# Pinning the order of every engine at the border between the up and the down projection of an encoder layer

## The chip, the cores and the metric

The kernel runs on one core of one Trainium2 chip. The metric is the device time of one execution in microseconds (us); lower is better. Engines are named as the profile names them: PE (TensorE, matrix products; PEld is its weight load), DVE (VectorE), ACT (ScalarE), POOL (GpSimd) and SP (SyncE, which here only issues DMA transfers).

## The reference, cut to what matters

One layer of a streaming encoder: a mixer (two kinds of attention, a gated MLP, an output projection, LayerNorm) and then the part that this document is about, a squared-ReLU MLP with a residual and a LayerNorm, on 1024 prompt tokens and 64 sample tokens, in float32:

```
def sq_relu_mlp(x, w_up, w_down):
    h = jnp.square(jax.nn.relu(jnp.einsum('btd,df->btf', x, w_up)))
    return jnp.einsum('btf,fd->btd', h, w_down)

xp = layer_norm(ALPHA * xp + sq_relu_mlp(xp, w_up[l], w_down[l]), ln2_g[l], ln2_b[l])
```

D_MODEL is 1024 and D_FF 4096, so w_up is 1024 x 4096 and w_down 4096 x 1024.

## The kernel before, in words

Both projections use Strassen-Winograd products: seven products in place of eight for a 2 x 2 split of rows, columns and depth. Each float32 operand is held as two halves of a rounded type, hi and lo: `split` (L1180 on) has ACT write hi, and DVE or POOL write lo = raw - hi. Every product takes three passes (hi x hi, hi x lo, lo x hi).

**The up part** runs over 16 pairs p of 256 columns of w_up. A pair has two token halves s, of 288 columns (s = 0, which carries half of the sample) and 256 columns (s = 1). One pair and half is a `Chain` (L1223): `product(i)` for i = 0 to 6 issues 12 matmuls into a PSUM bank A, B, C or D (the table PROD, L1219) and what takes the bank out. I write (14,1).6 for product 6 of pair 14, half 1. Products 0, 2 and 4 add up in bank A, and ACT copies the bank out after each of them (L1251), so product 2 waits for the copy after product 0, and product 4 for the copy after 2. Product 1 is added by DVE to the first copy (L1253). After product 5 DVE makes out(5) from bank D and the third copy (L1255), and out(3) from the third copy and bank C (L1256). Product 6 adds to bank D, so it waits for out(5); DVE then makes out(4) (L1258). `finish` (L1261) squares the four sums in place (L1265), makes four differences (L1271 to L1274), and SP stores the eight blocks to DRAM (h4_dr, h3_dr, hs_dr; L1275 to L1279). The copies lie in a tile `sn` of three slots, the blocks in a tile `hh`; each half has its own (tags sn0, sn1, hh0, hh1), and the next chain with that tag waits until the stores have read it. `prep(p)` loads a pair of w_up into the tile tagged `wr` and makes its operands; the x operands of half 1 lie in two tiles of the pool `big` (tag xw), those of half 0 in xo0.

**The down part** runs over 16 groups g = 2c + part. A group takes two pairs of h (q = 0, 1) against one row block of w_down (index c) for two token blocks x. `Down.product(n)` issues six matmuls of 512 columns, `Down.evac(n)` takes the bank out: ACT for n = 0 (L1587), DVE into the accumulators `acc` else (L1535, L1537, L1580). For each c and q, `wd_load` brings 1 MB of w_down (two transfers of 512 KB) into a raw tile, `wd_split` n = 0 to 6 makes seven hi and lo pairs (wset[0] lies in the two tiles `slots`, which take the place of the x operands of half 1; wset[1] lies in the pool dp on the right side, which is laid over what the up part used there), and `wd_sums` makes four differences in the raw tile between them. `h_load` brings h back from DRAM (into `awa` for the four-block part, `hr` for the three-block part), `h_split` makes its hi on ACT (L1396), copies it to PSUM on ACT (L1400), and has DVE write lo (L1401). `acc_load` loads the accumulators, which start as the mixer's result. `sample(c)` (L1614, L1616) does the sample tokens.

**What sets the order.** Each engine runs its instructions strictly in its own order, and a waiting instruction holds all behind it; so does SP with its transfers. A scheduler orders the instructions of the program when the kernel is built, from its own estimate of their times, with the earlier written ones preferred. `in_order()` (L99) is an exception: it links all instructions written inside it, engine by engine (SP too), in the order written. Before the change only the last part (c = 7 and the final LayerNorm, L1745 on) is pinned in this way.

**Around the border** (L1456 to L1502): after `prep(15)` the code writes chain (14,1), products 0 to 3 of (14,0), chain (15,1), then the allocation of `slots`, both `wd_load(0, q)` (q = 0 into `wr`, q = 1 into `hh1`), products 4 to 6 of (14,0), splits and sums, the loads of h and of accumulator 0, and chain (15,0) with more splits between its products. The loop of groups follows, all of it left to the scheduler. In the final part, `put_gb` (four ACT copies, L1728) stands before `squares(5)` (one ACT instruction with a sum, L1648), and `on_dve(5, ...)` (L1679, L1681) between the evacuations of the third chain.

## Time and profile before

| what | value |
|---|---|
| median of 3 runs | 1437.42 us (1433.44 to 1439.77) |
| profiled execution, its own time | 1441.04 us |
| its span in the profile | 1439.3 us |
| PE busy | 1340.2 us, 93% of the span |
| DVE, ACT, POOL busy | 1010.3, 720.3, 610.5 us |
| mean granted TensorE clock | 0.965 |
| up part, first and last matmul | 675.3 to 1063 us |
| down part, first and last matmul | 1044.9 to 1429 us |

The profile is of one execution, on the core's own time axis from the start of the span. A line of the timeline gives start, duration, engine, line of the program, operation, output and inputs by tile name, a count of merged instructions, and in brackets the idle time ahead of it with what ended it. A table by windows gives, for stretches of time, the length, the busy time and number of instructions per engine, then the mean granted clock of PE (1.00 is full), the share of the DMA engines and their GB/s. Merged matmul rows can carry the form of one of the two chains that they hold.

### The profile page before, as it was taken

What the parts mean: (1) busy time and instruction counts of PE and PEld (TensorE: products, weight loads), DVE (VectorE), ACT (ScalarE), POOL (GpSimd) and SP (SyncE); (2) the same over time, 40 slices, a digit from 0 to 9 for tenths busy, and PEclk for the clock granted to TensorE, in tenths of its full rate; (3) what the DMA queues carried; (4) which work ended last, traced back from release to release, by engine and by line L of the source; (5) the groups of instructions that cost most, each with busy time, mean ns of one, the idle gap of its engine ahead of it and who ended that gap; (6) DMA issues with size and microseconds to landing.
All of it is one profiled execution on the core that took longest, in us unless ns stands there. A gap on an engine that the chain in (4) does not pass through costs nothing.

```text
span 1439.3 us, 24229 instructions
## 1 busy us (share of the span) xinstructions
PE 1340.2 (93%) x8827; PEld 1217.8 (85%) x8827; DVE 1010.3 (70%) x1802; ACT 720.3 (50%) x1561; POOL 610.5 (42%) x660
## 2 busy tenths in 40 slices
PE   7999999999989988989879999999969999999996
PEld 6899999998988986867779999999947787787874
DVE  3567565767885699786736877876678667777766
ACT  3366565666564675233323222223335757667664
POOL 2222323266563537664322221222254556565555
PEclk9999999999999998989989999999978999999997
DMA  7324232322213434331124434334475334344433
GB/s 213 78 77 110 61 110 65 82 58 65 64 31 84 128 103 154 118 106 41 57 85 165 151 128 163 136 117 161 163 256 176 121 139 139 133 142 137 138 110 117
DMA packets 146208, 168.60 MB, mean 117 GB/s; under 512 B 27036, under 2 KB 112348, under 8 KB 146088
## 3 DMA queue, kind: packets, MB, share of 16 engines
q1 hardware_dynamic: 146088, 167.04, 37.0%
q8 instruction: 70, 1.15, 0.3%
q14 instruction: 50, 0.41, 0.1%
HBM read 109.00 MB, written 51.71 MB: 112 GB/s over the span
## 4 chain that ended last, share of the span: by engine, by line
PE 67%; DVE 9%; DMA 7%; ACT 7%; POOL 4%; issue 4%; SPq 1%; DVEq 0%; ACTq 0%; POOLq 0%
PE zA L1242 9%; PE mx L232 7%; PE zD L1242 6%; PE A L1570 6%; PE kvsb L337 5%; PE kvfox L337 4%; PE zB L1242 3%; PE zC L1242 3%; PE D L1570 3%; PE qsb L478 2%; DMA rd<-w_down 2%; PE qfox L478 2%; POOL wd L97 2%; PE Sfox L536 2%; PE B L1570 1%
## 5 line engine op out<-in xcount | busy, mean ns | idle before, releaser
L97 POOL TENSOR_TENSOR wa<-wr,wa 128x512 fp32r<-128x512 f32 x45 | 68.8, 1556 | 230.3 <-ACT wa L1182 230.3
L97 POOL TENSOR_TENSOR wd<-rd,wd 128x512 fp32r<-128x512 f32 x80 | 108.5, 1371 | 100.8 <-ACT wd L1182 96.5
L232 PE MATMUL mx<-xT,oTb 128*128 128x512 f32 (+1 forms) x416 | 108.8, 415 | 3.0 <-ACT oTb L191 2.0
L1242 PE MATMUL zA<-xo,ws 128*128 128x288 f32 (+1 forms) x720 | 96.7, 289 | 2.5 <-ACT sn L1251 2.5
L1242 PE MATMUL zD<-xo,ws 128*128 128x288 f32 (+1 forms) x720 | 98.3, 291 | 0.0
L232 PEld LDWEIGHTS mx<-xT,oTb 128*128 128x128 f32 (+1 forms) x416 | 78.7, 194 | 23.0 <-ACT oTb L191 2.9
L1251 ACT ACTIVATE sn<-zA 128x288 f32<-128x288 f32 (+1 forms) x96 | 37.7, 393 | 119.0 <-PE zA L1242 105.7
L1242 PEld LDWEIGHTS zA<-xo,ws 128*128 128x128 f32 x720 | 93.4, 189 | 3.0 <-ACT sn L1251 2.9
L1182 ACT ACTIVATE wd<-rd 128x512 fp32r<-128x512 f32 x112 | 67.6, 623 | 55.6 <-DMA rd<-w_down 25.1
L1242 PEld LDWEIGHTS zD<-xo,ws 128*128 128x128 f32 x720 | 94.9, 191 | 0.2
L337 PE MATMUL kvfox<-wkvfox,xT 128*128 128x256 f32 (+3 forms) x624 | 91.0, 295 | 3.1 <-DVE fx L440 2.0
L522 POOL TENSOR_TENSOR sgsb<-sgsb,snsb 128x127 f32<-128x127 f32 (+7 forms) x48 | 58.8, 1227 | 78.5 <-DVE snsb L520 67.6
L1570 PE MATMUL A<-wd,wd 128*128 128x512 f32 x312 | 86.9, 406 | 4.2 <-DVE acc L1537 3.4
L337 PE MATMUL kvsb<-wkvsb,xT 128*128 128x256 f32 (+1 forms) x624 | 87.7, 286 | 0.0
L337 PEld LDWEIGHTS kvfox<-wkvfox,xT 128*128 128x128 f32 (+1 forms) x624 | 82.1, 195 | 4.7 <-DVE fx L440 2.2
L1371 POOL TENSOR_TENSOR rd<-rd 128x512 f32<-128x512 f32 x56 | 79.8, 1425 | 10.7 <-DVE b L97 8.3
L520 DVE TENSOR_TENSOR_SCAN snsb<-snsb,one 128x128 f32<-128x128 f32 (+7 forms) x48 | 72.1, 1506 | 13.3 <-ACT snsb L519 12.7
L337 PEld LDWEIGHTS kvsb<-wkvsb,xT 128*128 128x128 f32 (+1 forms) x624 | 79.2, 187 | 0.2
L1570 PEld LDWEIGHTS A<-wd,wd 128*128 128x128 f32 x312 | 60.2, 195 | 20.7 <-issue 3.6
L1570 PE MATMUL A<-wd,h4a 128*128 128x512 f32 x240 | 68.3, 406 | 9.7 <-POOL wd L97 3.6
L1570 PEld LDWEIGHTS A<-wd,h4a 128*128 128x128 f32 x240 | 45.9, 193 | 22.8 <-POOL wd L97 4.4
L1438 ACT ACTIVATE ws<-wr 128x1024 fp32r<-128x1024 f32 x30 | 31.2, 1057 | 58.4 <-DVE wr L1192 58.4
(511 smaller groups left out, 3751.7 us busy)
## 6 DMA issues: line engine op xcount, KB each, us to landing
rd<-w_down SPq DMA_DIRECT2D x32, 512.0 KB, 4.4
awa<-h_dr SPq DMA_DIRECT2D x32, 512.0 KB, 4.3
wr<-w_up SPq DMA_DIRECT2D x15, 1024.0 KB, 5.5
h_dr<-hh SPq DMA_DIRECT2D x30, 512.0 KB, 3.2
hr<-h_dr SPq DMA_DIRECT2D x32, 384.0 KB, 3.5
h_dr<-hh SPq DMA_DIRECT2D x30, 384.0 KB, 3.5
raw<-w_in SPq DMA_DIRECT2D x44, 256.0 KB, 3.5
xr<-x_prompt SPq DMA_DIRECT2D x8, 512.0 KB, 6.9
```

Source lines behind the costliest of these rows:

```text
L97: eng.tensor_tensor(out, src, hi.bitcast(F32), op=ALU.subtract)
L232: nc.tensor.matmul(acc[0:m], oT[:, k, hx, 0:m], wo[k // 4][hw][:, k % 4, cs], start=(i == 0), stop=(i == len(seq) - 1))
L337: nc.tensor.matmul(acc[0:n, c0:c0 + n1 - n0], xT[k // 4][:, k % 4, c:c + n], wt[:, k, hw, n0:n1], start=(i == 0), stop=(i == len(seq) - 1))
L478: nc.tensor.matmul(acc[:, 0:w], wq[:, k, hw, :], xT[k // 4][:, k % 4, c:c + w], start=(i == 0), stop=(i == len(seq) - 1))
L520: nc.vector.tensor_tensor_scan(g[:, 0:n][:, ::-1], g[:, 0:n][:, ::-1], one.broadcast_to([P, n]), 1.0, op0=ALU.mult, op1=ALU.bypass)
L522: nc.gpsimd.tensor_tensor(s[:, 0:n - 1], s[:, 0:n - 1], g[:, 1:n], op=ALU.mult)
L1182: nc.scalar.activation(hi, raw, AF.Copy)
L1242: nc.tensor.matmul(z, w[:, hw, k], xop(s, bo, hx)[:, k, :], start=(new and k == 0 and j == 0), stop=(k == 3 and j == 2), skip_group_check= ...
L1251: nc.scalar.activation(sn[:, (0, None, 1, None, 2)[i], 0:n], z, AF.Copy)
L1371: eng.tensor_tensor(r[:, o], r[:, x], r[:, y], op=ALU.subtract)
L1438: nc.scalar.activation(ws[:, 0, q], raw[:, q], AF.Copy)
L1570: nc.tensor.matmul(z, h[:, hx, q, o], wset[self.c % 2][q][:, hw, wb], start=((n in (0, 3) or n == 1 and self.c == 0) and q == 0 and j == 0 ...
```

## The change

`in_order` gets an optional dictionary, so that a second pinned block goes on behind a first one on every engine. The border is one such block and the first group of down another, on the same dictionary.

Within the border the four chains run one behind another: (14,1), (15,1), (14,0), (15,0), with the last product of each put behind the first product of the next one. Chains of both halves alternate between the tag sets: (14,1) and (14,0) use sn1 and hh1, (15,1) and (15,0) use sn0 and hh0. `sn` has two slots in place of three, in all chains of the up part; the third copy is written by ACT straight to out(0) in `hh`. Both `wd_load(0, q)` go through `wr`, the second one behind the last split of the first. For q = 0 POOL does five of seven lo halves and DVE two; for q = 1 POOL does all seven. The first group of down is written out with its loads, splits and the last `finish`; the loop starts at g = 1, `sample(0)` moves from g = 0 to g = 1, and the operands `b12` of the sample are loaded by transfers of their own for c = 0 and for (1, 0) in g = 1.

In the final part `squares(5)` moves ahead of `put_gb`, each `on_dve(5, ...)` moves back by one place, and the small statistics tiles lie in the identity matrix, which is no longer needed by then.

```diff
     @contextmanager
-    def in_order():
+    def in_order(prev=None):
 
         traced = nc.cur_bb.bb.instructions
         last = traced[-1]
         yield
         at = next(k for k in reversed(range(len(traced))) if traced[k] is last) + 1
-        prev = {}
+        prev = {} if prev is None else prev
         for i in traced[at:]:
             p = prev.get(i.engine)
             if p is not None:
...
-        def product(self, i):
...
             if b == "A":
-                nc.scalar.activation(sn[:, (0, None, 1, None, 2)[i], 0:n], z, AF.Copy)
+
+                nc.scalar.activation(out(0) if i == 4 else sn[:, i // 2, 0:n], z, AF.Copy)
             elif b == "B":
                 add(out(2), z, sn[:, 0, 0:n], op=ALU.add)
             elif i == 5:
-                add(out(5), self.bank["D"], sn[:, 2, 0:n], op=ALU.add)
-                add(out(3), sn[:, 2, 0:n], z, op=ALU.subtract)
+                add(out(5), self.bank["D"], out(0), op=ALU.add)
+                add(out(3), out(0), z, op=ALU.subtract)
             elif i == 6:
                 add(out(4), z, sn[:, 1, 0:n], op=ALU.add)
-                self.finish(n)
-
-        def finish(self, n):
+                if rest:
+                    self.finish()
+
+        def finish(self):
             p, s = self.p, self.s
+            n = NS[s]
             for a, b in self.runs:
...
     def first_chain(s, weave):
-        sn = [sp.tile([P, 288], F32, name=f"sn0_{s}_{q}", tag="gl", bufs=3) for q in range(3)]
-
-        class Three:
...
     def wd_sums(c, q, eng):
 
+        for k in range(4):
+            wd_sum(c, q, k, eng)
+
+    def wd_sum(c, q, k, eng):
         r = raws[c, q]
-        for o, x, y in ((0, 1, 0), (1, 3, 1), (3, 3, 0), (2, 2, 3)):
-            eng.tensor_tensor(r[:, o], r[:, x], r[:, y], op=ALU.subtract)
+        o, x, y = ((0, 1, 0), (1, 3, 1), (3, 3, 0), (2, 2, 3))[k]
...
-            tag = only or ("o", "tr")[n_stage[0] % 2]
+            tag = (only or ("o", "tr"))[n_stage[0] % 2]
             n_stage[0] += 1
-            st = ps.tile([P, 4, P], F32, name=f"st{n_stage[0]}", tag=tag, bufs=1)[:, 0:o]
...
-        def chain(p, s):
-            sn = lp.tile([P, 3, NS[s]], F32, name=f"sn{p}_{s}", tag=f"sn{s}")
-            h8 = lp.tile([P, 8, NS[s]], F32, name=f"hh{p}_{s}", tag=f"hh{s}")
+        def chain(p, s, at=None):
+            at = s if at is None else at
+            sn = lp.tile([P, 2, NS[0]], F32, name=f"sn{p}_{s}", tag=f"sn{at}")
+            h8 = lp.tile([P, 8 * NS[0]], F32, name=f"hh{p}_{s}", tag=f"hh{at}")[:, 0:8 * NS[s]].rearrange(
+                "p (b c) -> p b c", b=8)
             return Chain(p, s, sn, lambda a, b: h8[:, a:b], ((2, 6),))
...
         prep(NP - 1)
-        c1, c0 = chain(NP - 2, 1), chain(NP - 2, 0)
-        for i in range(7):
-            c1.product(i)
-        for i in range(4):
-            c0.product(i)
...
+        q4 = [chain(NP - 2, 1, 1), chain(NP - 1, 1, 0)]
+        border = {}
+        with in_order(border):
+            for i in range(6):
+                q4[0].product(i)
+            wd_load(0, 0, "wr")
+            q4[1].product(0)
+            q4[0].product(6)
+            for i in range(1, 6):
+                q4[1].product(i)
+            q4.append(chain(NP - 2, 0, 1))
+            q4[2].product(0)
+            q4[1].product(6)
+            slots = [big.tile([P, 8704], F32R, name=f"wd0_{q}", tag="xw") for q in range(2)]
             for q in range(2):
-                wd_split(0, q, n, nc.gpsimd)
-        for q in range(2):
-            wd_sums(0, q, nc.vector)
-        h4 = lp.tile([P, 2, 2, 2, 4, P], F32R, name="h4a", tag="ws")
-        hbuf[0, 0], hbuf[0, 1] = h4[:, 0], h4[:, 1]
-        awa = lp.tile([P, 3, D], F32, name="awa", tag="wa")
-        hraw[0, 0], hraw[0, 1] = (awa[:, q].rearrange("p (o c) -> p o c", o=4) for q in range(2))
-        two(0, awa[:, 2])
-        for q in range(2):
-            h_load(0, 0, q)
-        h_load(0, 1, 1)
-        acc_load(0)
-        c0 = chain(NP - 1, 0)
-        for i in range(7):
-            c0.product(i)
-            if i in (0, 1, 2, 3):
-                for q in range(2):
-                    wd_split(0, q, i + 3, (nc.gpsimd, nc.vector)[q])
-            if i in (2, 4):
-                h_split(0, 0, i // 2 - 1, "tr")
-            if i == 4:
-                a45 = lp.tile([P, 2, D], F32, name="acc45", tag="hh1")
-                two(1, a45[:, 0])
-                two(4, a45[:, 1])
-                acc_load(1)
-                acc_load(4)
-            if i == 6:
-                h_load(0, 1, 0)
+                wset[0][q] = slots[q][:, 0:7168].rearrange("p (h b c) -> p h b c", h=2, b=7)
+                hbuf[1, q] = slots[q][:, 7168:8704].rearrange("p (h q o c) -> p h q o c", h=2, q=2, o=3)
+            q4[2].product(1)
+            wd_split(0, 0, 0, nc.gpsimd)
+            wd_split(0, 0, 2, nc.vector)
+            q4[2].product(2)
+            wd_sum(0, 0, 0, nc.vector)
+            wd_split(0, 0, 1, nc.gpsimd)
+            q4[2].product(3)
+            wd_sum(0, 0, 1, nc.vector)
+            wd_sum(0, 0, 2, nc.vector)
+            wd_split(0, 0, 4, nc.vector)
+            q4[2].product(4)
+            wd_sum(0, 0, 3, nc.vector)
+            wd_split(0, 0, 3, nc.gpsimd)
+            q4[2].product(5)
+            wd_split(0, 0, 5, nc.gpsimd)
+            wd_split(0, 0, 6, nc.gpsimd)
+            wd_load(0, 1, "wr")
+            q4.append(chain(NP - 1, 0, 0))
+            q4[3].product(0)
+            q4[2].product(6, False)
+            h4 = lp.tile([P, 2, 2, 2, 4, P], F32R, name="h4a", tag="ws")
+            hbuf[0, 0], hbuf[0, 1] = h4[:, 0], h4[:, 1]
+            awa = lp.tile([P, 3, D], F32, name="awa", tag="wa")
+            hraw[0, 0], hraw[0, 1] = (awa[:, q].rearrange("p (o c) -> p o c", o=4) for q in range(2))
+            two(0, awa[:, 2])
+            for q in range(2):
+                h_load(0, 0, q)
+            acc_load(0)
+            q4[2].finish()
+            h_load(0, 1, 1)
+            q4[3].product(1)
+            q4[3].product(2)
+            h_split(0, 0, 0, ("tr", "pt"))
+            q4[3].product(3)
+            wd_split(0, 1, 0, nc.gpsimd)
+            wd_split(0, 1, 1, nc.gpsimd)
+            q4[3].product(4)
+            h_split(0, 0, 1, ("tr", "pt"))
+            a45 = lp.tile([P, 2, D], F32, name="acc45", tag="hh1")
+            two(1, a45[:, 0])
+            two(4, a45[:, 1])
+            acc_load(1)
+            acc_load(4)
+            wd_sum(0, 1, 0, nc.vector)
+            wd_split(0, 1, 2, nc.gpsimd)
+            q4[3].product(5)
+            wd_sum(0, 1, 1, nc.vector)
+            wd_sum(0, 1, 2, nc.vector)
+            wd_split(0, 1, 3, nc.gpsimd)
+            q4[3].product(6, False)
+            h_load(0, 1, 0)
+            wd_split(0, 1, 4, nc.gpsimd)
+            wd_sum(0, 1, 3, nc.vector)
+            wd_split(0, 1, 5, nc.gpsimd)
+            wd_split(0, 1, 6, nc.gpsimd)
...
@@ -1512,18 +1548,6 @@
         for t in (5, 3, 7, NB):
             two(t, dp.tile([P, D], F32, name=f"acc{t}"))
         hs = dp.tile([P, 2, 2, 2, TS], F32R, name="hs")
-        a26 = lp.tile([P, 2304], F32, name="acc26", tag="hh0")
-        two(2, a26[:, 0:D])
-        two(6, a26[:, D:2 * D])
-        hsr = a26[:, 2 * D:2304].rearrange("p (q o c) -> p q o c", q=2, o=4)
-        for t in (5, 2, 6, 3, 7, NB):
-            acc_load(t)
-        for q in range(2):
-
-            r = dp.tile([P, 512], F32, name=f"rb{q}", tag="p1", bufs=2)
-            nc.sync.dma_start(r, w_dn[2 * q * P:(2 * q + 1) * P, 512:D])
-            split(b12[q][:, 0], b12[q][:, 1], r, nc.gpsimd)
-        hs_load(0)
...
         def norm(t):
             if t not in lst:
-                lst[t] = dp.tile([P, 16], F32, name=f"lstb{t}", tag="lst", bufs=NT)
+
+                lst[t] = ident[:, 16 * t:16 * t + 16] if t < NB else dp.tile([P, 16], F32, name="lstb")
             return lst[t]
...
+        def b12_again(c, q):
+
+            r = dp.tile([P, 512], F32, name=f"rb{c}_{q}", tag="p1", bufs=2)
+            k = 2 * (2 * c + q)
+            nc.sync.dma_start(r, w_dn[k * P:(k + 1) * P, 512:D])
+            split(b12[q][:, 0], b12[q][:, 1], r, nc.gpsimd)
+
+        def first_group():
+            ch = [Down(0, x) for x in range(2)]
+
+            def both(n):
+                for d in ch:
+                    d.product(n)
+                for d in ch:
+                    d.evac(n)
+
+            acc_load(5)
+            for q in range(2):
+                h_load(1, 0, q)
+            both(0)
+            q4[3].finish()
+            both(1)
+            wd_load(1, 0)
+            h_split(0, 1, 0)
+            both(2)
+            h_split(0, 1, 1)
+            for q in range(2):
+                h_load(1, 1, q)
+            both(3)
+            for k in range(3):
+                wd_split(1, 0, k, nc.gpsimd)
+            for t in (2, 6, 3, 7, NB):
+                acc_load(t)
+            h_split(1, 0, 0)
+            both(4)
+            wd_sums(1, 0, nc.gpsimd)
+            both(5)
+            h_split(1, 0, 1)
+            wd_split(1, 0, 3, nc.vector)
+            wd_split(1, 0, 4, nc.gpsimd)
+            both(6)
+            wd_split(1, 0, 5, nc.vector)
+            wd_split(1, 0, 6, nc.gpsimd)
+
+        a26 = lp.tile([P, 2304], F32, name="acc26", tag="hh0")
+        two(2, a26[:, 0:D])
+        two(6, a26[:, D:2 * D])
+        hsr = a26[:, 2 * D:2304].rearrange("p (q o c) -> p q o c", q=2, o=4)
+        with in_order(border):
+            first_group()
         for c in range(NC - 1):
             for part in range(2):
                 g = 2 * c + part
+                if g == 0:
+                    continue
+                if g == 1:
+                    hs_load(0)
+                    for q in range(2):
+                        b12_again(0, q)
                 wd_load(c + 1, part)
                 ch = [Down(g, x) for x in range(2)]
...
-                    if n == 3 and part == 0:
+                    if n == 3 and (part == 0 or g == 1):
                         sample(c)
+                        if g == 1:
+                            b12_again(1, 0)
...
@@ -1800,21 +1883,21 @@
             shift(1)
             do(2, 1)
             h_split(g + 1, 1, 1)
+            squares(5)
             put_gb()
-            squares(5)
             normalize(1)
             times(1)
             do(2, 2)
-            on_dve(5, 0, 0)
             ch[3].preload()
             do(2, 3)
+            on_dve(5, 0, 0)
+            do(2, 4)
             on_dve(5, 1, 0)
-            do(2, 4)
-            on_dve(5, 0, 1)
             do(2, 5)
             neg_mean(2)
+            on_dve(5, 0, 1)
+            do(3, 0)
             on_dve(5, 1, 1)
-            do(3, 0)
             squares(2)
```

## The prediction, made before the changed kernel had run

> **What bounds the kernel now.** I read the engine shares first, then the stretches of the border, then each engine's timeline there.
>
> ```profile
> PE 1340.2 (93%) x8827; PEld 1217.8 (85%) x8827; DVE 1010.3 (70%) x1802; ACT 720.3 (50%) x1561; POOL 610.5 (42%) x660
> PEclk9999999999999998989989999999978999999997
> PE 67%; DVE 9%; DMA 7%; ACT 7%; POOL 4%; issue 4%; SPq 1%; DVEq 0%; ACTq 0%; POOLq 0%
> ```
>
> PE bounds nearly all of it, and from 1100 to 1380 us it is busy for 279.3 of 280 us. What another order can give is PE's idle time and its lowered clock. The stretches of the border (length, busy us and count on PE, PEld, DVE, ACT, POOL, then clock, DMA share, GB/s):
>
> ```profile
> 1030.00:1045.00 15.00, 15.00 (x118) 15.00 (x118) 10.63 (x13) 7.62 (x16) 8.91 (x6) 1.00 0.40 133
> 1045.00:1060.00 15.00, 7.47 (x39) 5.92 (x38) 9.76 (x18) 4.38 (x10) 2.96 (x2) 0.91 0.76 261
> 1060.00:1075.00 15.00, 9.00 (x27) 6.81 (x27) 10.63 (x9) 7.22 (x14) 11.18 (x8) 0.61 0.96 313
> 1075.00:1090.00 15.00, 12.04 (x32) 8.49 (x31) 13.08 (x17) 7.54 (x15) 6.34 (x6) 0.57 0.69 245
> 1090.00:1100.00 10.00, 10.00 (x45) 7.73 (x44) 7.25 (x12) 3.82 (x8) 4.28 (x5) 1.00 0.25 86
> ```
>
> From 1045 to 1090 us there are 98 matmuls: 37 of up (288 columns, 24 in 3.04 us, so 0.127 each) and 61 of down (512 columns, 6 in 1.40 us, 0.23 each). At full clock they take 4.7 + 14.0 = 18.7 us; they took 45. So **26.3 us** are lost there. The waits behind it, and the second lossy place, at the end:
>
> ```profile
> 1059.09 1.65 PE L1570 MATMUL B<-wd,h4a 128*128 128x512 f32 x3 [4.08 <-DVE hh L1253]
> 1072.34 2.07 PE L1570 MATMUL A<-wd,h4a 128*128 128x512 f32 x4 [3.63 <-POOL wd L97]
> 1082.01 2.93 PE L1570 MATMUL A<-wd,h4a 128*128 128x512 f32 x6 [2.42 <-ACT p L1587]
> 1409.64 2.90 PE L1570 MATMUL A<-wd,wd 128*128 128x512 f32 x6 [3.18 <-DVE acc L1537]
> 1413.17 2.93 PE L1570 MATMUL lastD<-wd,wd 128*128 128x512 f32 x6 [0.63 <-DVE acc L1537]
> ```
>
> Six matmuls take 2.7 us there in place of 1.4: half clock. The weights came late because the heads of two queues stood waiting for (15,0).6 with splits of already landed weights behind them, on ACT and on POOL:
>
> ```profile
> 1063.71 1.67 ACT L1182 ACTIVATE wd<-rd 128x512 fp32r<-128x512 f32 x3 [8.92 <-PE zD L1242]
> 1063.74 0.95 POOL L1414 MEMSET acc<- 64x1024 f32 x1 [15.79 <-PE zD L1242]
> ```
>
> In two-microsecond stretches (PE busy, clock, DMA share, GB/s) the clock shows when it steps:
>
> ```profile
> 1057.00:1059.00 2.00, 0.00 (x0) 0.58 1.00 307
> 1063.00:1065.00 2.00, 1.62 (x6) 0.71 0.68 178
> 1067.00:1069.00 2.00, 1.71 (x4) 0.64 0.93 323
> 1087.00:1089.00 2.00, 2.00 (x8) 0.74 1.04 394
> ```
>
> Read as a mix of 1.00 and 0.50 these put the steps at 1057.3 (down), 1064.2 (up), 1067.6 (down) and 1088.0 (up): multiples of 3.4 us apart. A 3.4 us window in which PE was busy for 28 to 33% ended in half clock, windows of 47 and 54% did not, and it took a fully busy window to come back (one of 81 to 84% did not do it). So a gap costs itself, and if some 2.2 us of it fall in one window, another 1.7 to 3.4 us after it (half of 3.4 to 6.8 us), 2.6 on average.
>
> **The change, part by part.** Times below are on the trace's axis; after 1007.3 us, where (14,1) starts, they are forecasts. A product of 12 takes 1.42 us with 256 columns, 1.52 with 288.
>
> *The third copy goes to out(0).* ACT now has to wait for hh1, whose stores by (13,1) were issued late:
>
> ```profile
> 1014.84 0.33 SPq L1275 DMA_DIRECT2D h_dr<-hh  x1
> 1015.78 0.33 SPq L1276 DMA_DIRECT2D h_dr<-hh  x1
> 1030.57 0.42 DVE L1253 TENSOR_TENSOR hh<-zB,sn 128x256 f32<-128x256 f32 x1 [3.31 <-DMA h_dr<-hh]
> ```
>
> The last row resumed 3.28 us after its store's issue (1027.29), so hh1 is free at 1019.1. Then the copy (0.39), two DVE adds (0.42 each, partly beside it) and (14,1).6 can go at 1020.4. Before, products of (14,0) filled this; now six products and (15,1).0 end at 1017.4. **Gap 1: 3.0 us**, with 6 in 10 chances that 2.2 us of it fall in one window, so I add 2.6. Bounds: 0 (the stores land sooner, 2.1 us being the shortest such transfer here, and DVE is not behind) to 8 (DVE takes the waiting add ahead of the 7.5 us in which it makes the operands of pair 15). The Trainium skill, TensorE: Matmul & The Clock Gate, section Part 1, says that PE falls to half clock after at least one idle window of some 3.4 us; by that, gap 1 would stay warm and the sum come out 2.6 us better. The rows above differ: a window that was 28% busy was enough.
>
> *The chains one behind another.* (15,1).6 then ends at T = 1020.4 + 11.5 + 2.6 = 1034.5, and `slots` is free. From T: POOL's and DVE's work for q = 0 is a chain, since a sum waits for a split's lo and a later split for the sum. POOL needs 1.3 us per lo alone (1.29 in the last group), and a DVE operation with both inputs in SBUF waits while POOL has one: the four differences of (15,0) took 1.37 to 1.50 us beside POOL, 0.41 elsewhere. `finish` of (15,1) on DVE goes to T+3.7, sums 1 and 2 to 7.9, sum 3 to 9.1; POOL's five end at 6.1 (second), 10.4, 11.7, 13.3. So out(5) of (14,0) is ready at 9.5 where PE is at 9.1: 0.5 us, and (14,0).6 ends at 11.1.
>
> *Loads.* SP is pinned: `wd_load(0, 1)` needs `wr`, free at T+13.3 (1047.8; before, it went to hh1 at 1047.98), and `h_load(0, 0, q)` stands behind it, though `awa` is free at 11.2. The first `wd_load` before (1 MB, issued 1019.8) had its bytes moved from 1021 to 1024. So w_down moves from T+14.7 to 17.8, h to 21.0. Then ACT, in its pinned order: hi, copy, hi, copy for x = 0 (0.55 each), two splits of q = 1, the copy after (15,0).4, four more for x = 1: T+26.2. DVE then: the last lo (0.7), a sum (0.6), out(5): **(15,0).6 starts at T+28.1**. PE's other work ends at 11.1 + 5 x 1.52 = 18.7. **Gap 2: 9.4 us, and 2.6** of half clock behind it. Lower bound 6 (loads as quick as the 4.3 us median, no collisions of DVE and POOL), upper 14 (each DVE difference at 1.4 us).
>
> *The first group.* Its weights for n = 0 and 1 are there, the others come from POOL by T+38 in the order of use. DVE is the tight one: out(4), a sum, `finish` (7.5 us for (15,0) beside a busy POOL, 1063.7 to 1071.2), then evacuations and lo halves; (n = 4) needs them at T+44.6 and gets them at 44.6. SP's queue holds stores, accumulators and h ahead of `wd_load(1, 0)`; it lands at T+45 and is needed in g = 2. For evacuations that come just late I count 1.5 us; bounds 0 and 5.
>
> *Costs at nothing.* POOL does two more lo halves and two more of b12, 6 us in some 45 of which it is busy about 30. The 16 sample matmuls only move. One load of 256 KB more: DMA is under half busy after 1100 us. Two slots of `sn`: the same instructions; in pair 0 the 3.35 us wait at 716.5 for the stores of the first chain can grow by one copy, 0.4 us.
>
> *The final part.* `squares(5)` (1.13 us) no longer waits for `put_gb` (2.32 us), and DVE evacuates (2,3) before it meets `on_dve(5, 0, 0)`, which waited 2.27 us for `squares(5)`. The 3.18 us gap stays (its evacuation stands behind `h_split`, unmoved); the 0.63 us gap goes, and with it the broken window that kept the clock at half from 1409.6 to 1419.1 (4.75 us lost). Left: 2.6. Gain 0.6 + 2.2 = **2.8 us**; bounds 0.6 and 4. The work moved back falls into DVE's idle 2.64 us at 1420.
>
> **Sum.** After: 3.0 + 2.6 + 0.5 + 9.4 + 2.6 + 1.5 = 19.6 lost, before 26.3: 6.7, and 2.8 at the end: 9.5 us. Against the profiled execution's 1441.0 that is 1431.5; it lies 3.6 above the median of 1437.4, from which I get 1427.9.
>
> **Rivals.** (a) *Gaps close further*: gap 1 stays warm, gap 2 is 6 us, the first group runs through: 2.6 + 3.4 + 1.5 more, 1420. For it: DMA reached over 400 GB/s in stretches of the trace. Of this, that gap 1 alone leaves the clock up has a chance of 0.4, since it falls across two windows that often, and gives 9.5 + 2.6 = 12.1 us, 1425.3, within the forecast's own range. (That is also what the clock rule of the Trainium skill, TensorE: Matmul & The Clock Gate, Part 1, would make of it.) (b) *The wait is only moved*: hh1 late with DVE's order against it (5 more) and gap 2 at 13: 9.5 - 8.6, 1436.5. For it: DVE and POOL did collide in every difference of (15,0). (c) *Slower*: the first group never gets warm. Before, gaps of 0.5 to 3.6 us kept half clock from 1067.6 to 1088.0; if DVE's evacuations, pinned behind `finish` and the lo halves, leave a gap of 0.6 us in each window, its 84 matmuls take 38.6 us in place of 19.3. That is 16.7 beyond the 2.6 counted, plus five gaps: 9.5 - 19.7, 1447.6. It decides once evacuations lag PE by over 1.4 us. Against it: some 19 us of DVE work stand in 24.
>
> **How the numbers follow.** About 0.5% (7.2 us) can be told from no change here. Forecast 0.48 (1423 to 1434, two thirds of it past 0.5%), (a) 0.26, (b) 0.13, (c) 0.13. Faster 0.32 + 0.26 = 0.58, same 0.16 + 0.13 = 0.29, slower 0.13. Range 1417 (all low bounds, less 3 of scatter) to 1438 (gap 1 at 8, gap 2 at 14).
>
> **What would show it.** Right: a PE gap near 3 us ended by out(0)'s copy or out(5) before (14,1).6, the long gap before (15,0).6 with h's loads in its chain, full clock through most of g = 0, no 0.63 us gap near the end. Wrong: h landed before (15,0).3, so that gap 2 is short; or gaps inside g = 0; or g = 2 waiting for weights.

## The result and the profile after

The changed kernel takes 1428.53 us (median of 6 runs, 1426.93 to 1430.65), the kernel before 1437.24 (6 runs): ratio 0.9943, 95% interval 0.9922 to 0.9964. A second comparison, beside later experiments, gave 1430.31 against 1438.94: 0.9948 [0.9931, 0.9966]. So it is 7.5 to 8.7 us faster, where 9.5 was forecast. The profiled execution took 1429.89 us (span 1428.2); that of before 1441.04.

Engine shares, clock and chain of waits of after:

```profile
PE 1333.8 (93%) x8827; PEld 1214.6 (85%) x8827; DVE 1001.7 (70%) x1799; ACT 720.9 (50%) x1561; POOL 613.6 (43%) x663
PEclk9999999999999998999979999999999999999998
PE 61%; DVE 11%; DMA 8%; ACT 7%; POOL 6%; issue 6%; SPq 1%; DVEq 0%; ACTq 0%; POOLq 0%
```

The mean clock went from 0.965 to 0.970, and PE's busy time fell by 6.4 us with the same 8827 matmuls: fewer of them ran at half clock. The stretches of the border (columns as before):

```profile
1030.00:1045.00 15.00, 15.00 (x116) 14.87 (x115) 10.32 (x17) 5.47 (x11) 6.04 (x5) 1.00 0.16 63
1045.00:1060.00 15.00, 9.12 (x58) 8.64 (x56) 6.40 (x11) 6.72 (x13) 3.52 (x3) 0.79 0.81 270
1060.00:1075.00 15.00, 12.87 (x61) 10.53 (x60) 14.58 (x19) 6.01 (x13) 8.43 (x5) 0.98 0.79 274
1075.00:1090.00 15.00, 12.48 (x52) 9.48 (x53) 10.20 (x17) 11.58 (x23) 10.64 (x9) 1.00 0.97 329
1090.00:1100.00 10.00, 10.00 (x45) 8.19 (x44) 10.00 (x18) 7.79 (x16) 6.38 (x6) 1.00 0.71 251
```

Between 1060 and 1090 us the clock was 0.61 and 0.57 before and is 0.98 and 1.00 now. PE's gaps in the border and in the final part, from PE's timeline:

```profile
1020.20 2.93 PE L1242 MATMUL zD<-xo,ws 128*128 128x256 f32 x12 [2.94 <-DVE hh L1256]
1056.85 3.25 PE L1242 MATMUL zC<-xo,wa 128*128 128x288 f32 x12 [5.88 <-DVE h4a L1408]
1061.53 1.86 PE L1242 MATMUL zD<-xo,ws 128*128 128x288 f32 x12 [1.43 <-DVE hh L1256]
1076.01 0.93 PE L1594 MATMUL A<-wd 128*128 128x512 f32 x3 [1.71 <-DVE awa L1559]
1083.62 0.97 PE L1594 MATMUL A<-wd,h4b 128*128 128x512 f32 x3 [1.47 <-DVE h4b L1408]
...
1401.73 2.75 PE L1594 MATMUL A<-wd,wd 128*128 128x512 f32 x6 [3.20 <-DVE acc L1561]
1404.28 2.04 PE L1594 MATMUL lastD<-wd,wd 128*128 128x512 f32 x6
```

These are gap 1 ahead of (14,1).6, gap 2 in two pieces ahead of (15,0).5 and .6, two gaps of the first group, and the one left in the final part; the old 0.63 us gap behind it is gone. Two-microsecond stretches (length, PE busy, clock, DMA share, GB/s) show the half clock of both border gaps:

```profile
1019.00:1021.00 2.00, 0.80 (x3) 0.65 0.25 45
1021.00:1023.00 2.00, 2.00 (x11) 0.50 1.00 397
1023.00:1025.00 2.00, 2.00 (x18) 0.99 0.21 82
...
1055.00:1057.00 2.00, 0.15 (x1) 0.50 1.07 384
1057.00:1059.00 2.00, 2.00 (x9) 0.50 0.93 310
1059.00:1061.00 2.00, 1.10 (x5) 0.61 0.59 144
1061.00:1063.00 2.00, 1.47 (x11) 1.00 0.95 373
```

Behind gap 1 it lasts to 1023.0, one window of 3.4 us. At gap 2 about half of it lies inside the idle time, and the first group starts at full clock.

**How traces are compared.** No edit touches what comes ahead of (14,1).0, yet its start lies anywhere from 1004.5 to 1010.5 us in the traces below. So I measure from there (S) to the start of product lastB of the third final chain (E): 394.3 us before (1007.33 to 1401.60), 386.6 after (1007.04 to 1393.68), 388.2 in a second trace of the changed kernel (1006.05 to 1394.25). A second trace with the old border, that of the kernel before with the new final part below, gives 394.0. The border's gain is thus **5.8 to 7.6 us**. From E to the start of the last product it is 26.0 before, and 22.7 and 21.2 after.

### The profile page after: what moved, and what is told of

It is laid out like the page before. It is cut to its first block, busy times and chain, and to the rows that moved or that the text cites. A ratio compares the mean times of both kernels' runs of the same rounds, so it can differ in the third digit from the quotient of the medians.

```text
span 1428.2 us, 24304 instructions
## 1 busy us (share of the span) xinstructions
PE 1333.8 (93%) x8827; PEld 1214.6 (85%) x8827; DVE 1001.7 (70%) x1799; ACT 720.9 (50%) x1561; POOL 613.6 (43%) x663
## 4 chain that ended last, share of the span: by engine, by line
PE 61%; DVE 11%; DMA 8%; ACT 7%; POOL 6%; issue 6%; SPq 1%; DVEq 0%; ACTq 0%; POOLq 0%
PE zA L1242 9%; PE zD L1242 6%; PE mx L232 6%; PE kvsb L337 5%; PE kvfox L337 5%; PE A L1594 4%; DMA rd<-w_down 3%; PE zB L1242 3%; PE zC L1242 3%; POOL wd L97 2%; DMA awa<-h_dr 2%; PE qfox L478 2%; POOL rd L1378 2%; PE D L1594 2%; PE Sfox L536 2%
## 5 line engine op out<-in xcount | busy, mean ns | idle before, releaser
L1182 ACT ACTIVATE wd<-rd 128x512 fp32r<-128x512 f32 x112 | 67.6, 624 | 61.5 <-POOL rd L1378 28.4
L520 DVE TENSOR_TENSOR_SCAN snsb<-snsb,one 128x128 f32<-128x128 f32 (+7 forms) x48 | 72.2, 1507 | 13.3 <-ACT snsb L519 12.7
L1594 PE MATMUL A<-wd,h4a 128*128 128x512 f32 x240 | 65.3, 394 | 0.4 <-ACT p L1611 0.2
L1252 ACT ACTIVATE sn<-zA 128x288 f32<-128x288 f32 (+1 forms) x64 | 25.1, 393 | 80.3 <-PE zA L1242 70.0
L1242 PE MATMUL zA<-xo,wa 128*128 128x288 f32 (+1 forms) x360 | 50.0, 293 | 10.2 <-ACT wa L1182 10.2
```

The costliest lines, as they stand in the source:

```text
L520: nc.vector.tensor_tensor_scan(g[:, 0:n][:, ::-1], g[:, 0:n][:, ::-1], one.broadcast_to([P, n]), 1.0, op0=ALU.mult, op1=ALU.bypass)
L1182: nc.scalar.activation(hi, raw, AF.Copy)
L1242: nc.tensor.matmul(z, w[:, hw, k], xop(s, bo, hx)[:, k, :], start=(new and k == 0 and j == 0), stop=(k == 3 and j == 2), skip_group_check= ...
L1594: nc.tensor.matmul(z, h[:, hx, q, o], wset[self.c % 2][q][:, hw, wb], start=((n in (0, 3) or n == 1 and self.c == 0) and q == 0 and j == 0 ...
```

## The experiments

| kernel | median us (runs) | ratio to before [95%] | S to E | E to last product |
|---|---|---|---|---|
| changed kernel, second time | 1430.31 (10) | 0.9948 [0.9931, 0.9966] | 388.2 | 21.2 |
| before + new final part | 1438.13 (10) | 0.9997 [0.9978, 1.0015] | 394.0 | 22.6 |
| after, old final part | 1431.85 (10) | 0.9955 [0.9938, 0.9973] | 386.7 | 24.9 |
| own slot for the third copy | 1432.64 (1) | - | 388.9 | 22.7 |
| h's loads first | 1426.32 (4) | 0.9914 [0.9884, 0.9943] | 380.9 | 24.0 |
| two products ahead | 1424.04 (6) | 0.9913 [0.9894, 0.9932] | 382.5 | 22.7 |
| h first, and ACT's order | 1424.42 (6) | 0.9914 [0.9895, 0.9934] | 381.3 | 22.7 |
| first group's order | 1436.56 (12) | 0.9983 [0.9967, 1.0000] | 392.7 | 24.0 |
| all three edits | 1426.46 (6) | 0.9923 [0.9898, 0.9947] | 383.1 | 22.7 |
| two ahead + h first | **1422.22** (6) | **0.9891** [0.9872, 0.9911] | 377.8 | 23.8 |
| the same + ACT's order | 1422.45 (5) | 0.9887 [0.9869, 0.9904] | 378.9 | 22.7 |
| first group not pinned | 1431.02 (4) | 0.9950 [0.9931, 0.9970] | 389.4 | 22.7 |

### The final part, alone and left out

The change's last hunk was put into the kernel before (as below), and taken out of the changed one.

```diff
-            put_gb()
             squares(5)
+            put_gb()
...
-            on_dve(5, 0, 0)
             ch[3].preload()
             do(2, 3)
-            on_dve(5, 1, 0)
+            on_dve(5, 0, 0)
             do(2, 4)
-            on_dve(5, 0, 1)
+            on_dve(5, 1, 0)
...
```

> The kernel before with the change of the final part alone (squares(5) ahead of put_gb, on_dve(5) one place later). If the final part's share of the gain is what I worked out (the 0.63 us gap goes, and half clock after the 3.2 us gap lasts one window of 3.4 us or a little more in place of 9.5 us), the time is 2.8 us below the kernel before (between 0.6 and 4) and the trace shows no gap ahead of product 5 of the third chain. Rival: the shorter half clock in the changed kernel's trace is luck of the window's phase; then the gap goes but the time falls by 0.6 us only. Rival: the gain at the end comes from the border (another phase); then nothing changes here.

> The changed kernel with the final part as it was. If border and final part add up: slower than the changed kernel by 2.8 us (0.6 to 4), so 6 us (0.4%) faster than the kernel before, which is the border alone; the 0.63 us gap is back ahead of product 5 of the third chain. If the border gave it all: no loss against the changed kernel.

The gap rows of the kernel before with the new final part, then of the changed one with the old:

```profile
1410.53 2.90 PE L1570 MATMUL A<-wd,wd 128*128 128x512 f32 x6 [3.20 <-DVE acc L1537]
1413.22 1.73 PE L1570 MATMUL lastD<-wd,wd 128*128 128x512 f32 x6
```

```profile
1403.52 1.64 PE L1594 MATMUL A<-wd,wd 128*128 128x512 f32 x6 [3.20 <-DVE acc L1561]
1407.05 1.71 PE L1594 MATMUL lastD<-wd,wd 128*128 128x512 f32 x6 [1.89 <-DVE acc L1561]
1408.56 4.50 PE L1594 MATMUL A<-wd,wd 128*128 128x512 f32 x12
```

The edit does what was said: the second gap goes. But its worth hangs on where the windows lie. In the second kernel the clock stayed up through the 3.20 us gap (six products in 1.64 us) and fell after the second one, which is 1.89 us and not 0.63 since the six products ahead of it ran faster. The new final part took 21.2, 22.6 to 22.7, or 23.8 to 24.0 us in the traces: no half clock, one window, two. The old took 24.9 and 26.0. In time it is worth 0.4 us by the ratio when put into the kernel before (0.9997), and 1.0 to 1.7 when taken out of the changed one (0.9955 against 0.9948 and 0.9943); no interval tells either from nothing. That of the first runs from 3.2 us faster to 2.2 us slower, so the 2.8 us forecast for the final part are neither shown nor excluded; the median lies nearer to the rival that gives it 0.6 us. The border carries most of the gain.

### What makes gap 1

The third copy of (14,1) and (15,1) gets a slot of its own again:

```diff
-                nc.scalar.activation(out(0) if i == 4 else sn[:, i // 2, 0:n], z, AF.Copy)
+                third = sn[:, 2, 0:n] if self.own else out(0)
+                nc.scalar.activation(third if i == 4 else sn[:, i // 2, 0:n], z, AF.Copy)
...
```

The two adds that read the copy are changed with it, and `sn` of these two chains has three slots of 256 columns.

> The changed kernel, but the third copy of (14,1) and (15,1) goes to a slot of its own in sn (three slots of 256 columns) and not to out(0) in hh1. Theory of the prediction: the 2.94 us gap ahead of (14,1).6 comes from this copy's wait for hh1; then the copy runs at about 1014.5 us and the gap shrinks to some 2.5 us at least, to nothing if the copy alone made it. Rival: the gap is made by DVE, whose 2.29 us operation for pair 15 and whose add to out(2), which lies in hh1 too, stand ahead of out(5); then the copy runs early and the gap stays at 2.9 us.

Rows of ACT and DVE ahead of gap 1 in the changed kernel, then of ACT, DVE and PE with the slot of its own:

```profile
1018.76 0.39 ACT L1252 ACTIVATE hh<-zA 128x256 f32<-128x256 f32 x1 [1.60 <-DMA h_dr<-hh]
1017.19 2.29 DVE L97 TENSOR_TENSOR ws<-wr,ws 128x2048 fp32r<-128x2048 f32 x1 [1.14 <-ACT ws L1445]
1019.40 0.42 DVE L1254 TENSOR_TENSOR hh<-zB,sn 128x256 f32<-128x256 f32 x1
1019.74 0.41 DVE L1256 TENSOR_TENSOR hh<-zD,hh 128x256 f32<-128x256 f32 x1
```

```profile
1017.53 0.36 ACT L1254 ACTIVATE sn<-zA 128x256 f32<-128x256 f32 x1
1018.87 2.29 DVE L97 TENSOR_TENSOR ws<-wr,ws 128x2048 fp32r<-128x2048 f32 x1 [1.41 <-ACT ws L1448]
1021.41 0.41 DVE L1259 TENSOR_TENSOR hh<-zD,sn 128x256 f32<-128x256 f32 x1
1021.88 2.93 PE L1243 MATMUL zD<-xo,ws 128*128 128x256 f32 x12 [4.08 <-DVE hh L1259]
```

The copy no longer waits for a DMA, and the gap is 4.08 us. What ended last in both is DVE: its 2.29 us operation on pair 15's operands stands ahead of out(2) and out(5). These two write to the same `hh1` as the copy, but its stores did not decide either: in the changed kernel they had let the copy go at 1018.76, and DVE reached out(2) only at 1019.40. With the slot of its own the gap is even longer, since ACT's early copies now stand between the two halves of pair 15's operands that DVE's operation waits for; it starts 11.3 us after S, against 10.2 and 10.8 in the two traces of the changed kernel. So the copy's wait did not make the gap; this rests on one trace and one timed run of this kernel.

The second test of gap 1 gives PE more to do ahead of it: product 1 of (15,1) before product 6 of (14,1).

```diff
             q4[1].product(0)
+            q4[1].product(1)
             q4[0].product(6)
-            for i in range(1, 6):
+            for i in range(2, 6):
```

> Change: product 1 of the second quarter of (15,1), 12 matmuls, is put ahead of product 6 of (14,1). Theory A (gap 1 of 2.94 us is the time by which the split of the low part on DVE is late, and the half clock behind it comes from the share of the window that stands idle): the products 0 and 1 of (15,1) together give some 2.9 us of work between (14,1).5 and (14,1).6 in place of 1.45, so the gap shrinks to about 1.5 us, no window falls under a third busy, the clock stays up, and (15,1).6 ends 2.5 to 3 us earlier; the time is 1 to 3 us under the changed kernel's, about 1426. Theory B (the clock falls after any gap of this length, also one of 1.5 us): the product comes forward by 1.4 us and the half clock stays. Theory C (the wait is a chain that is as late as its own last link, which moves with the products): the gap stays at 2.9 us, since DVE takes up the extra work of product 1's addition ahead of it; nothing is won.

Gap 1 in the second trace of the changed kernel, then with this edit:

```profile
1019.88 2.93 PE L1242 MATMUL zD<-xo,ws 128*128 128x256 f32 x12 [3.61 <-DVE hh L1256]
```

```profile
1021.56 1.69 PE L1242 MATMUL zD<-xo,ws 128*128 128x256 f32 x12 [2.19 <-DVE hh L1256]
```

Theory A holds. DVE's operation starts 10.8 us after S in both of these traces, 0.7 us later than in the first trace of the changed kernel (one of DVE's differences ahead of it took 1.50 us, not 0.41), and the gap is 1.42 us shorter, which is the one product put in front. The clock stayed at 1.00 through it: (14,1).6 took 1.69 us, not 2.93. S to E fell by 4.1 us against the first trace, the median by 4.5 against the first comparison of the changed kernel. That is more than the 1 to 3 us forecast: 2.0 us of it are there when (15,1).6 starts, the rest came behind it. In the three kernels below that have the same edit among others the gap is 1.51, 2.32 and 2.65 us; behind the last of these half clock is back (12 matmuls in 2.77 us). It shows that gap 1 is work missing on PE against a release fixed by DVE, and that the half clock behind it is a second price for the same idle time.

### What makes gap 2

The two transfers of `h_load(0, 0, q)` go ahead of `wd_load(0, 1, "wr")` on SP:

```diff
-            wd_load(0, 1, "wr")
             q4.append(chain(NP - 1, 0, 0))
...
             for q in range(2):
                 h_load(0, 0, q)
+            wd_load(0, 1, "wr")
```

> The changed kernel with the two loads of h ahead of the second load of w_down on SP. Theory: the long wait before (15,0).5 and .6 (9.1 us in all) is the landing of h, behind 1 MB of w_down on the queue and behind the release of wr; then h's loads are issued 2 us earlier (once awa is free, about 1044.6) and land 4 to 5 us earlier, near 1049, and the first hi of h runs there. ACT's next instructions are splits of w_down that now lands 3 us later, near 1053, with the copy after (15,0).4 behind them, so only part of this reaches PE: (15,0).6 starts 3 to 5 us earlier. Rival: the wait hangs on DVE and POOL's chain and not on the transfers; then (15,0).6 moves by less than 1 us.

SP and ACT in the changed kernel, then SP, ACT and PE with h first:

```profile
1046.02 0.81 SPq L1360 DMA_DIRECT2D rd<-w_down  x2
1046.88 0.91 SPq L1393 DMA_DIRECT2D awa<-h_dr  x2
1053.57 0.63 ACT L1403 ACTIVATE h4a<-awa 128x512 fp32r<-128x512 f32 x1 [5.32 <-DMA awa<-h_dr]
```

```profile
1040.86 0.80 SPq L1393 DMA_DIRECT2D awa<-h_dr  x2
1045.56 1.20 SPq L1360 DMA_DIRECT2D rd<-w_down  x2
1052.62 0.63 ACT L1182 ACTIVATE wd<-rd 128x512 fp32r<-128x512 f32 x1 [1.95 <-DMA rd<-w_down]
1053.16 0.39 ACT L1252 ACTIVATE hh<-zA 128x288 f32<-128x288 f32 x1
1050.90 1.86 PE L1242 MATMUL zC<-xo,wa 128*128 128x288 f32 x12 [0.39 <-DVE h4a L1408]
1057.62 3.25 PE L1242 MATMUL zD<-xo,ws 128*128 128x288 f32 x12 [4.87 <-DVE hh L1256]
```

Against S, h is asked for 5 us earlier though w_down is not asked for later, and the stop ahead of (15,0).5 shrinks from 5.88 to 0.39 us. The forecast cause of gap 2 is shown. What is left (4.87 us) is the next link: ACT's copy after (15,0).4 stands behind a split of w_down that waits 1.95 us for its landing, and behind the copy come the split of h (0,0,1) on ACT and DVE and then out(5), which releases (15,0).6. By the ratios (0.9914 against 0.9943 and 0.9948) it is 0.3% under the changed kernel, with intervals that overlap; S to E is 5.7 us less, of which 1.3 are small gaps of the later groups (below).

The next edit takes this link away too: the copy and `h_split(0, 0, 1)` ahead of the splits of w_down (0,1).

```diff
-            wd_split(0, 1, 0, nc.gpsimd)
-            wd_split(0, 1, 1, nc.gpsimd)
             q4[3].product(4)
-            h_split(0, 0, 1, ("tr", "pt"))
...
+            q4[3].product(5)
+            h_split(0, 0, 1, ("tr", "pt"))
+            wd_split(0, 1, 0, nc.gpsimd)
+            wd_split(0, 1, 1, nc.gpsimd)
             wd_sum(0, 1, 0, nc.vector)
```

> Change: the loads of h go ahead of the second load of w_down as in the run before, and in ACT's, DVE's and POOL's set order the copy after (15,0).4, with the split of h (0,0,1), comes ahead of the two splits of w_down (0,1). Theory A (gap 2 is made of two links in series, the loads of h behind the load of w_down, and then ACT's copy behind its split of w_down): with both gone (15,0).6 comes at 1054 to 1055 where the changed kernel has it at 1061.5 and the loads alone 1057.6; gap 2 falls to 1 to 3 us; the splits of (0,1) come 2 to 4 us later than there, and the first group of down waits for them by 0 to 3 us. Time 3 to 6 us under the changed kernel's, 1423 to 1426. Theory B (the first group of down cannot start before the last splits of w_down (0,1) on POOL, so that what gap 2 gives comes back as a gap in the first group): (15,0).6 comes earlier as above, but the first group loses it again at its products 4 to 6, and the time is that of the run with the loads alone, 1426.

```profile
1058.83 2.11 PE L1594 MATMUL A<-wd,h4a 128*128 128x512 f32 x8 [0.64 <-POOL wd L97]
1065.82 3.03 PE L1594 MATMUL A<-wd,h4a 128*128 128x512 f32 x12 [2.16 <-ACT p L1611]
1075.48 1.62 PE L1594 MATMUL A<-wd 128*128 128x512 f32 x3 [3.91 <-DVE awa L1559]
```

This is Theory B. There is no idle time left in (15,0), and the first group starts 6.5 us earlier against S than with h first alone (47.8 us after it, not 54.2); all of it comes back in the rows shown and in a half clock behind the last. ACT's evacuation stands behind splits that wait for DVE's sums, and DVE's evacuation behind the `finish` of (15,0). The median, 1424.42, lies where Theory A put it, but the ratio is that of h first alone (0.9914 both), and S to E is no shorter (381.3 against 380.9).

### The first group

Its gaps of 1.71 and 1.47 us were attacked by writing `finish` of (15,0) behind `both(3)`, the split of h (1,0,0) ahead of the splits of w_down (1,0), and the loads of accumulators 3 and 7 ahead of `finish`; then by this together with two products ahead and h first with ACT's order.

```diff
             both(0)
-            q4[3].finish()
             both(1)
...
+            for t in (3, 7):
+                acc_load(t)
+            q4[3].finish()
+            h_split(1, 0, 0)
             for k in range(3):
                 wd_split(1, 0, k, nc.gpsimd)
...
```

> Change: in the first group of down alone, the finish of (15,0) comes after both(3), the split of h (1,0,0) ahead of the loads and splits of w_down (1,0), and the accumulator loads 3 and 7 ahead of the finish. Theory A (the gaps of 1.71 and 1.47 us in and behind the first group are the finish of (15,0) ahead of the evacuations on DVE, and ACT's split of h (1,0,0) behind a split of w_down that waits for its load): both gaps go, 3 us, and the time is 2 to 3 us under the changed kernel's, about 1426. Theory B (the wait moves on): the finish comes later, so h's last blocks are stored and loaded again later, and the second group waits for them instead; 0 to +2 us.

> Change: the three edits together: product 1 of (15,1) ahead of product 6 of (14,1); loads of h first and the copy ahead of the splits; the first group's order. If each gap is a place of its own, the gains add up to 2.8 + 6 + 3 = 12 us at most, 1417 to 1420, ratio to the kernel before 0.986 to 0.988. If the border has one long chain (w_down's and h's loads and splits) that ends in the first group, the earlier gains come back as waits there, and the time is 1423 to 1426, that of the best single edit.

The first misses both of its theories (1436.56). All three edits together (1426.46; S to E 383.1) come out near the second theory and no better than two products ahead alone. Gap rows of the first of the two, from later groups that the edit does not touch:

```profile
1180.53 1.17 PE L1594 MATMUL A<-wd,h4b 128*128 128x512 f32 x4 [0.47 <-DVE acc L1561]
1273.38 0.96 PE L1594 MATMUL D<-wd 128*128 128x512 f32 x3 [1.16 <-DVE acc L1561]
1363.67 0.95 PE L1594 MATMUL D<-wd 128*128 128x512 f32 x3 [1.31 <-DVE acc L1561]
```

The gaps of the first group shrank to 0.90 us. But the groups from g = 1 on are ordered by the scheduler, and with another first group it chose another order for all engines there. Read from the traces instruction by instruction, the order after 1100 us is that of the changed kernel with the old final part, the own slot and two products ahead; it is another in all other kernels of the table that have the new border, those with h first among them. The gaps between 1100 and 1397 us (without the 3.2 us one) add up to 6.3 us in this kernel and 4.9 with all three edits, against 2.1 and 1.4 in the two traces of the changed kernel and 0.9 with h first. In this trace half clock also reached from the stop ahead of (15,0).5 (from 1059 us) to 1069, through (15,0).6 (3.25 us, not 1.86) into the first group. With a gap 1 of 3.77 us these come to some 7 us, less 3.2 us of shorter gaps in gap 2 and the first group: 4 of the 6.1 us by which S to E is longer; the rest is not placed. So neither theory was it: the wait did not move to g = 1, the order of everything later did. That this order, and not the later `finish` or the moved loads, is the cause of the small gaps is argued from the traces; an edit with the later order held fixed was not tried.

One part of the change undone alone: the first group left to the scheduler.

```diff
-        with in_order(border):
-            first_group()
+        first_group()
```

> Change: one part undone alone: the first group of down is no longer held in its written order; the planner then puts 12 of its matmuls ahead of (15,0).5 and more ahead of (15,0).6. Theory A (the pin matters, since the planner counts w_down's splits as ready when they are not): TensorE waits for POOL's splits with the last two products of (15,0) queued behind, its finish comes later, and the border loses 4 to 10 us: 1432 to 1439. Theory B (these matmuls only fill gap 2, where TensorE is idle for 7 us): 2 to 4 us earlier, 1424 to 1426. Theory C (the first group's share of the change is nothing): 1427 to 1430.

```profile
1052.23 1.22 PE L1594 MATMUL A<-wd,h4a 128*128 128x512 f32 x2 [3.12 <-ACT h4a L1403]
1072.47 1.19 PE L1594 MATMUL A<-wd,h4b 128*128 128x512 f32 x2 [3.88 <-DVE awa L1561]
```

The time is that of the changed kernel (1431.02 against 1430.31 beside it, nearest to Theory C), but as a sum of things: the group's matmuls fill gap 2 (3.12 us are left of 7.3), a stop of 3.88 us comes instead within the group, and the gaps after 1100 us add up to 5.9. Pinning the first group is worth nothing measurable by itself.

### The two winning edits together

> The changed kernel as it stands, for a comparison on one chip with the three that follow. Both theories: 1427 to 1431 and a ratio of 0.992 to 0.996. From the start of (14,1).0 to the start of the third chain's last product lastB of the last f pairs its first trace took 386.6 us; a second trace tells how much of that moves from run to run by itself: under 1 us if the order decides, 2 to 4 us if the place of the clock's windows does.

> Change: the two edits that won by themselves, together: product 1 of (15,1) ahead of product 6 of (14,1), and the loads of h ahead of the second load of w_down. Theory A (gap 1 and gap 2 are places of their own): from (14,1).0 to lastB it took 382.5 and 380.9 us with one of them against 386.6 in the changed kernel, so 376.8 with both; the time is 1418.5 to 1421. Theory B (both meet in the same next limit, the finish of (15,0) on DVE and the splits of w_down's second load, which set when the first group gets on): 380 to 382, the time 1423 to 1426.

> Change: as the kernel before, and the copy after (15,0).4 and the split of h (0,0,1) ahead of the splits of w_down (0,1). Theory B (the first group waits for DVE's finish and for the splits): no idle time ahead of (15,0).6, but 5 to 7 us in the first group ahead of its third and fifth product; the time within 1 us of the kernel before. Theory A: 2 to 4 us under it.

```profile
1018.23 1.69 PE L1242 MATMUL zD<-xo,ws 128*128 128x256 f32 x12 [1.51 <-DVE hh L1256]
1046.70 1.85 PE L1242 MATMUL zC<-xo,wa 128*128 128x288 f32 x12 [0.40 <-DVE h4a L1408]
1053.30 3.25 PE L1242 MATMUL zD<-xo,ws 128*128 128x288 f32 x12 [4.75 <-DVE hh L1256]
```

S to E is 377.8 us, near the 376.8 that Theory A gives; the median of 1422.22 lies between the two forecasts. Both gaps are places of their own. Against the changed kernel in the same comparison this is 8.1 us less, with intervals that lie apart, and 1.1% under the kernel before: it beats both. Some 0.5 to 1.3 us of it lie in the later groups, whose gaps after 1100 us add up to 0.9 us here, as with h first. ACT's order adds nothing to it either (1422.45): as its Theory B says, the stops come back in the first group, 0.64, 2.17 and 2.27 us.

## Why the prediction was right

The forecast was 1427.9 with a gain of 9.5 us: 6.7 in the border and 2.8 at the end. Measured are 7.5 to 8.7 us, 5.8 to 7.6 of it in the border by the traces.

- **Full clock through the first group: right**, and the largest part of the gain. PE is busy for 12.9 and 12.5 us of the two stretches that had 9.0 and 12.0 at a clock near 0.6. Rival (c) did not come, nor the warm gap 1 of rival (a): half clock followed gap 1 in all seven traces in which nothing ahead of it is edited.
- **Gap 1: 2.94 us against 3.0, the reason wrong.** The step "ACT now has to wait for hh1" names a true wait (1.60 us) that decided nothing; DVE's operand work ahead of the adds did, which the prediction named only in its bounds. That the size came out is luck: in the seven traces the gap lies between 2.93 and 3.77 us (3.61 in the second trace). The half clock was put at 2.6 us: (14,1).6 lost 1.35 in the first trace; in the second the clock came back only after 1025 us, and two products lost 2.5. Both windows that the rule allowed occurred.
- **T and the loads: right.** (15,1).6 ended at 1033.1 (forecast 1034.5), `wd_load(0, 1)` was issued at T+12.9 (13.3), h was there at T+20.5 (21.0), and (14,0).6 lost 0.15 us (0.5).
- **Gap 2: its end right, its split not.** (15,0).6 started at T+28.4 (forecast 28.1) in the first trace and at T+29.7 in the second. 5.88 + 1.43 us of idle time and 1.5 us of half clock in (15,0).5 make 8.8 against 9.4 + 2.6; the second trace has 8.6 of idle time and 4.5 of half clock. The stop was forecast ahead of (15,0).6 alone. Most of it came one product earlier, since product 5 takes the PSUM bank (tag pt) that `h_split(0, 0, 0)` now stages h in; the step had counted ACT and DVE but not the bank. This let (15,0).5 run inside the cold window, and the 2.6 behind the gap fell away in the first trace; in the second, half clock reached through (15,0).6 into the first group (12 matmuls in 4.36 us in place of 2.9).
- **First group: 1.5 forecast, 3.2 idle in the first trace and 0.9 in the second.** One stop was the evacuation behind `finish`, foreseen; the other, ACT's split of h behind splits of w_down (1,0) that wait for landing, was not.
- **Final part: 2.8 forecast; 3.3 in the first pair of traces, 0.4 to 1.7 by the ratios.** The mechanism was right, the size depends on where the windows lie.
- **The sum**: the items of the first trace come to some 16.5 us lost (19.6 forecast), which would leave a border gain of 9.6 where S to E shows 7.6. Longer gaps after 1100 us (2.1 against 1.3) are 0.8 of the difference; the rest is not placed. The items of the second trace come to 20.4, a gain of 5.7 where S to E shows 6.1. So the forecast lies between the two traces.
- **A slip**: a row of 24 merged matmuls was taken as 288-column ones throughout, but holds both widths; 12 of 288 columns take 1.59 us, not 1.52. It moves the loss of before from 26.3 to 26.1.
- **Not priced**: the scheduler's order of the groups after the pinned part, whose gaps add up to 0.9 to 6.3 us in the traces above.

On the clock, the Trainium skill (TensorE: Matmul & The Clock Gate, Part 1) asks for an idle window of some 3.4 us before PE slows down. By that gap 1 (2.94 us) would have stayed warm; the half clock behind it in the first trace, and behind the same gap of 2.95 us with h first, says otherwise, and so the reading of the windows from before's trace was the better one. The same part of the Trainium skill says that the window runs freely and that the place of a step therefore varies from run to run; the traces agree (one or two windows of half clock, or none, behind the same gap).

## What to carry to other kernels

When a pinned order leaves a gap, ask first which engine ends last there and whether another product can be put in front: one line for gap 1 and one for gap 2 gave as much again as the whole change. Removing a wait pays only down to the next link of its chain, here SP's queue, then ACT's, then DVE's. And where a scheduler orders what follows an edit, compare that part too, since an edit that closes 2 us of gaps can open 4 us elsewhere.

## What the runs showed of the hardware

- The same 3.2 us gap in the final part left the clock up in two of the fourteen traces, was followed by 3.4 us of half clock in eight and by 6.8 us in three; in the kernel before, with the 0.63 us gap behind it, by 10.2 us. Ahead of (14,1).6, gaps of 1.51, 2.19 and 2.32 us left it up; 2.65 us and more did not. This fits windows of 3.4 us on a raster of their own: in each trace every stretch of half clock up to the last matmul lasts 3.41 us or a whole multiple of it and starts a whole multiple after the others, and two windows that share a 3.2 us gap evenly are each 53% busy, where in the trace of before windows of 28 to 33% fell to half clock and those of 47 and 54% did not.
- One kernel moves by several us from run to run: the changed kernel from 1426.05 to 1435.43 in 10 runs. In the traces the start of the border alone moved by 6 us with the same code ahead of it. That it is the windows' place against the gaps of the earlier parts is likely, not shown.
- In the changed kernel's trace three of DVE's four differences of 256 columns in `finish` of (15,0) took 1.40 us beside POOL's splits, the fourth, behind them, 0.41; with the 2.45 us ahead of them that is 7.1 us in one piece, and evacuations of the first group wait behind it (the 1.71 us gap).
